# Two output parts to a pass, and conditioning loads spread evenly between the weight loads, in the first half of a gated short-convolution layer

## The chip, the cores and the metric

The kernel runs on one core of one Trainium2 chip. The number that counts is the device time of one execution in microseconds. Three timed executions of the kernel before took 926.06, 925.84 and 923.97 us, so the median is 925.84 us. Another execution was recorded by the hardware profiler; its span, from the first to the last instruction, is 925.9 us. All times "at" a point are counted from the start of that span.

## The reference

One layer is computed for 256 tokens of 2048 features; everything is float32.

```
h = rmsnorm(x, norm_g)                                    # x: 256 x 2048
mod = silu(c) @ ada_w + ada_b                             # 2048 -> 3 * 2048: shift, scale, gate
h = h * (1 + scale) + shift
b_gate, c_gate, v, g = split(h @ w_in, 4)                 # w_in: 2048 x (4 * 4096)
u = causal_depthwise_conv(c_gate * v, conv_w)             # 3 taps
y = b_gate * u * silu(g)
out = rmsnorm(x + gate * (y @ w_out), final_g)            # w_out: 4096 x 2048
```

The weights are large for so few tokens: `w_in` has 134 MB, the shift and scale columns of `ada_w` 33.5 MB, its gate columns 16.8 MB and `w_out` 33.5 MB. Each is read once.

## The kernel before

**Products.** For float32 accuracy a weight tile `raw` is split into a rounded part `hi` (ScalarE, ACT, L324) and the rest `lo` (VectorE, DVE, L325), and the activations h into `hT` the same way. A product of a 128x128 weight tile is then three matmuls on TensorE (PE, L419): hi by the rounded h, hi by the rest of h, lo by the rounded h. So after its first two matmuls a pass needs `lo`, which needs `hi`, which needs the load.

**Features come in groups.** The 2048 features are 16 feature tiles (k). A tile of h can be used once its scale and shift are known, and these are sums over all of `ada_w`'s rows. They are made on DVE: each load `at` of `ada_w` (a piece of 512 KB, issued as two DMAs of 256 KB, L388) is multiplied by silu(c) and added to `gv` by two instructions (L399 for the first of a group, else L401). Eight pieces make a group of two feature tiles; the first group is made in the start-up, seven more follow while products already run. When a group's `gv` is whole, PE turns it (`tp_g`, L408), ACT sums it (L410), and `modulate` writes `hT` for these two tiles (L309 to L318).

**The early stage.** The first half of the output channels is 16 parts: 4 chunks of channels `ch` by 4 quarters `q` (the four outputs of `w_in`), each of 512 columns. A part needs all 16 feature tiles, but they come one group after another, so a part is computed in several passes: `part(ch, q, k0, k1, seed)` takes tiles k0 to k1. A pass has one PSUM tile `mm_s` (two banks; the pool of 3 such tiles fills six of the eight banks). It loads `raw_s` (L462) with up to four feature tiles by 512 columns: 1 MB, or 512 KB for two feature tiles. The pool for `raw` has three buffers of 1 MB, those for `hi` and `lo` three each, that for `at` four. At the end `keep` brings the sums to SBUF: ACT copies them (L440) when it is the part's first pass, or when the pass was seeded, that is when ACT had copied the sums so far into PSUM before it (L452); else DVE adds them (L442).

**What sets the order.** `plan()` runs on the host and lists the passes and the `ada` pieces. It keeps four running times (load, PE, DVE, ACT) with fixed costs for each, and puts a piece before a pass when its estimate says that loading has room (`fill`). The tile framework then orders the instructions of each engine by priority and by its own estimate of time; DVE's `gv` instructions have a lower priority (`later(GIVE)`), so a `lo` may pass them. Within an engine the order is then fixed. All of the weight and `ada_w` loads are issued by one queue, SyncE's (SP), in its order.

After 3072 matmuls on `mm_s` the second half of the channels follows with all features ready (`mm_b`, loads `raw` of eight feature tiles by 256 columns), then the output product (`mm_o`). These stages aren't touched by the change.

Of the kernel before, what the change touches and what calls it, by code (L numbers as in the profile page):

```python
# [13 lines left out]
P = 128  # L14
D = 2048
E = 4096
# [35 lines left out]
def plan():  # L52

# [7 lines left out]
    burst = SLOT // P  # L61

    def ada():
        nonlocal load, dve
        k0, nk, i = pieces.pop(0)
        steps.append(("ada", k0, nk, i))
        load = max(load, dve - AAHEAD) + ALOAD
        dve = max(dve, load + 2.0) + VPIECE
        if i == 4 * nk - 1:
            ready.extend([dve + ALAG] * nk)  # L70

    def products(n, need):

        nonlocal load, pe, dve, act
        load = max(load, pe - WAHEAD)
        pe = max(pe, need, load + min(n, burst) * LOAD + WLAG) + n * PRODUCTS
        load += n * LOAD
        act = max(act, load + 2.0) + n * SBLOCK
        dve = max(dve, load + 2.0) + n * VBLOCK

    def fill():

        while pieces and max(load, dve - AAHEAD) + ALOAD + burst * LOAD + WLAG < pe:
            ada()

    order = [(ch, q) for ch in range(NCH) for q in QUARTERS]
    new = list(order)
    while new or any(k < KT for k in done.values()):
        fill()
        hi = sum(r <= pe for r in ready)  # L90
        if new:
            p = new.pop(0)
            done[p] = 0
        else:
            old = [p for p in order if done[p] < KT]
            p = old[0] if hi == KT else min(old, key=lambda p: done[p])
            while hi == done[p]:
                while len(ready) == hi:
                    ada()
                pe = max(pe, ready[hi])  # L100
                hi = sum(r <= pe for r in ready)
        products((hi - done[p]) * CT, ready[hi - 1])
        seed = done[p] > 0 and act < dve
        if done[p] == 0:
            act += SCOPY
        elif seed:
            act += SSEED
        else:
            dve += VSUM
        steps.append(("mm", *p, done[p], hi, seed))  # L110
        done[p] = hi
    while pieces:
        ada()
# [4 lines left out]
def short_conv_layer(ctx: ExitStack, tc: tile.TileContext, x, c, norm_g, ada_w, ada_b, w_in, conv_w, w_out, final_g, out):  # L118
# [325 lines left out]
    def part(ch, q, k0, k1, seed):  # L444


        col = q * E + ch * CT * P
        step = SLOT // (CT * P)
        first = k0
        bank = psum.tile([P, CT, T], F32, tag="mm", name="mm_s")  # L450
        if seed:
            nc.scalar.copy(bank, acc[ch, q])  # L452
        if pieces0:
            for k in range(NK0):
                chunk_products(bank, *pieces0[k], 0, k, k0, k1, late=True)
            pieces0.clear()
            k0 = NK0
        for s0 in range(k0, k1, step):
            sk = min(step, k1 - s0)
            n = sk * CT * P  # L460
# [25 lines left out]
    LATER = (4, 7, 10)  # L486
    whole = [0] * NCH
    for kind, *step in plan():
        if kind == "ada":
            ada_piece(*step)  # L490
        else:
            ch, k1 = step[0], step[3]
            part(*step)
            if step[2] == 0 and len(acc) in LATER:
                k = 4 + 4 * LATER.index(len(acc))
                with tc.issue_after(last_mm[0].ins), behind(ended):
                    turn_x(k, k + 4)
                    if k == 4:
                        turn(rows2, 0, 96, cw)
# [206 lines left out]
```

## Time and profile before

| | |
|---|---|
| median of three timed runs | 925.84 us |
| span of the profiled execution | 925.9 us |
| PE busy | 904.4 us, 98% of the span |
| DVE busy | 613.9 us |
| ACT busy | 472.8 us |
| first matmul on `mm_s` | 26.50 us |
| end of the `mm_s` products in the chain that ended last | 394.35 us |
| loads moved by SP's queue | 226.51 MB |

A row of the grouped view names line, engine, operation, what is written and read, and a count; then the busy time, the mean of one in ns, and the time that the engine idled just before these instructions, with what ended it. In the list of waits the three numbers are the time in total, how often, and the longest. In a timeline row the first two numbers are start and duration, and a bracket tells an idle time before and what ended it. Rows of stretches give, for each engine, busy time and (x) the number of instructions that began in it, then the granted clock of TensorE as a share, the share of DMA time and the rate in GB/s.

### The profile page before, as it was taken

What the parts mean: (1) busy time and instruction counts of PE and PEld (TensorE: products, weight loads), DVE (VectorE), ACT (ScalarE), POOL (GpSimd) and SP (SyncE); (2) the same over time, 40 slices, a digit from 0 to 9 for tenths busy, and PEclk for the clock granted to TensorE, in tenths of its full rate; (3) what the DMA queues carried; (4) which work ended last, traced back from release to release, by engine and by line L of the source; (5) the groups of instructions that cost most, each with busy time, mean ns of one, the idle gap of its engine ahead of it and who ended that gap; (6) DMA issues with size and microseconds to landing.
All of it is one profiled execution on the core that took longest, in us unless ns stands there. A gap on an engine that the chain in (4) does not pass through costs nothing.

```text
span 925.9 us, 16464 instructions
## 1 busy us (share of the span) xinstructions
PE 904.4 (98%) x7119; PEld 869.6 (94%) x7119; DVE 613.9 (66%) x604; ACT 472.8 (51%) x465; POOL 0.7 (0%) x6
## 2 busy tenths in 40 slices
PE   7999899999999999999999999999999999999996
PEld 6999899999999999999999999999999988888885
DVE  5889888898486799875554455445554544545882
ACT  3787776675557856644434433443334433444333
POOL 0000000000000000000000000000000000000000
PEclk9999999999999999999999999999999999999999
DMA  9999999999895789776655665666556496566542
GB/s 314 355 367 355 367 329 338 350 365 358 268 306 186 219 297 357 243 231 201 202 186 188 199 204 184 189 199 204 183 183 195 140 348 226 186 200 205 182 137 92
DMA packets 163753, 227.66 MB, mean 246 GB/s; under 512 B 5680, under 2 KB 104160, under 8 KB 163296
## 3 DMA queue, kind: packets, MB, share of 16 engines
q1 hardware_dynamic: 163440, 226.51, 74.0%
q8 instruction: 56, 0.92, 0.4%
q14 instruction: 17, 0.14, 0.0%
q10 hardware_dynamic: 240, 0.09, 0.0%
HBM read 224.49 MB, written 2.10 MB: 245 GB/s over the span
## 4 chain that ended last, share of the span: by engine, by line
PE 88%; DMA 6%; DVE 3%; issue 1%; SPq 1%; ACT 1%; ACTq 0%; DVEq 0%
PE mm_b L419 38%; PE mm_s L419 31%; PE mm_o L604 6%; PE mm_o L605 6%; PE mm_o L603 6%; DMA at<-in_ada_w_dram 3%; DMA raw_s<-in_sc_w_in_dram 2%; DVE gv L401 1%; DVE lo L325 1%; DMA x<-in_x_dram 1%; SPq L212 0%; ACT hi L324 0%; PE ps_gate L542 0%; PE tp_g L408 0%; SPq L388 0%
## 5 line engine op out<-in xcount | busy, mean ns | idle before, releaser
L419 PE MATMUL mm_s<-hT,hi 128*128 128x256 f32 x2048 | 352.9, 278 | 0.1
L419 PE MATMUL mm_b<-hT,hi 128*128 128x256 f32 x2048 | 348.8, 276 | 0.0
L419 PEld LDWEIGHTS mm_s<-hT,hi 128*128 128x128 f32 x2048 | 310.4, 189 | 1.2 <-issue 0.5
L419 PEld LDWEIGHTS mm_b<-hT,hi 128*128 128x128 f32 x2048 | 308.4, 188 | 0.2 <-issue 0.2
L419 PE MATMUL mm_s<-hT,lo 128*128 128x256 f32 x1024 | 284.4, 279 | 6.8 <-DVE lo L325 6.7
L419 PE MATMUL mm_b<-hT,lo 128*128 128x256 f32 x1024 | 282.6, 276 | 0.0
L325 DVE TENSOR_TENSOR lo<-raw,hi 128x2048 fp32r<-128x2048 f32 (+1 forms) x66 | 148.1, 2244 | 135.1 <-ACT hi L324 135.1
L324 ACT CAST hi<-raw 128x2048 fp32r<-128x2048 f32 (+1 forms) x66 | 123.7, 1874 | 208.5 <-PE mm_b L419 150.2
L419 PEld LDWEIGHTS mm_s<-hT,lo 128*128 128x128 f32 x1024 | 193.1, 189 | 7.6 <-DVE lo L325 7.6
L419 PEld LDWEIGHTS mm_b<-hT,lo 128*128 128x128 f32 x1024 | 192.2, 188 | 0.2 <-issue 0.2
L325 DVE TENSOR_TENSOR lo<-raw_s,hi 128x2048 fp32r<-128x2048 f32 (+1 forms) x80 | 147.9, 1849 | 40.5 <-ACT hi L324 39.7
L324 ACT CAST hi<-raw_s 128x2048 fp32r<-128x2048 f32 (+1 forms) x80 | 124.6, 1557 | 67.6 <-PE mm_s L419 49.8
L325 DVE TENSOR_TENSOR lo<-raw_o,hi 128x2048 fp32r<-128x2048 f32 x32 | 73.3, 2291 | 65.1 <-ACT hi L324 65.0
L324 ACT CAST hi<-raw_o 128x2048 fp32r<-128x2048 f32 x32 | 61.0, 1907 | 107.2 <-PE mm_o L605 85.0
L604 PE MATMUL mm_o<-lo,y 128*128 128x512 f32 x256 | 99.7, 391 | 0.0
L603 PE MATMUL mm_o<-hi,y 128*128 128x512 f32 x256 | 99.3, 389 | 0.0
L605 PE MATMUL mm_o<-hi,y 128*128 128x512 f32 x256 | 99.3, 389 | 0.0
L401 DVE SCALAR_TENSOR_TENSOR gv<-at,silu_c,gv 128x512 f32<-128x512 f32 x105 | 78.6, 749 | 9.2 <-DMA at<-in_ada_w_dram 7.8
L440 ACT COPY acc<-mm_s 128x1024 f32<-128x1024 f32 x54 | 54.4, 1010 | 35.1 <-PE mm_s L419 34.9
L605 PEld LDWEIGHTS mm_o<-hi,y 128*128 128x128 f32 x256 | 48.0, 188 | 10.1 <-issue 0.2
L604 PEld LDWEIGHTS mm_o<-lo,y 128*128 128x128 f32 x256 | 48.0, 188 | 10.1 <-issue 0.2
L603 PEld LDWEIGHTS mm_o<-hi,y 128*128 128x128 f32 x256 | 48.0, 188 | 10.0
(94 smaller groups left out, 375.4 us busy)
## 6 DMA issues: line engine op xcount, KB each, us to landing
raw<-in_sc_w_in_dram SPq DMA_DIRECT2D x64, 1024.0 KB, 5.7
raw_s<-in_sc_w_in_dram SPq DMA_DIRECT2D x47, 1024.0 KB, 7.8
raw_o<-in_sc_w_out_dram SPq DMA_DIRECT2D x32, 1024.0 KB, 5.2
at<-in_ada_w_dram SPq DMA_DIRECT2D x114, 256.0 KB, 7.3
raw_s<-in_sc_w_in_dram SPq DMA_DIRECT2D x33, 512.0 KB, 5.8
at_g<-in_ada_w_dram SPq DMA_DIRECT2D x32, 512.0 KB, 8.0
at<-in_ada_w_dram SPq DMA_DIRECT2D x6, 512.0 KB, 8.8
x<-in_x_dram SPq DMA_DIRECT2D x4, 512.0 KB, 6.1
```

What stands on the lines that cost most here:

```text
L324: nc.scalar.copy(hi[:, :n], raw[:, :n])
L325: nc.vector.tensor_tensor(out=lo[:, :n], in0=raw[:, :n], in1=hi[:, :n].bitcast(F32), op=ALU.subtract)
L401: nc.vector.scalar_tensor_tensor(out=gv, in0=at4[:, i], scalar=c_k, in1=gv, op0=ALU.mult, op1=ALU.add)
L419: mm = last_mm[0] = nc.tensor.matmul(dst, w, h[:, k], start=begins and left, stop=ends, skip_group_check=True)
L440: nc.scalar.copy(acc[ch, q], bank)
L603: nc.tensor.matmul(po, yh, hi[:, o], start=opens, stop=False, skip_group_check=True)
L604: nc.tensor.matmul(po, yh, lo[:, o], start=False, stop=False, skip_group_check=True)
L605: nc.tensor.matmul(po, yl, hi[:, o], start=False, stop=ct == NCT - 1, skip_group_check=True)
```

## The change

Two neighbouring parts (the same quarter, chunks 0 and 1 or 2 and 3) go through a pass together. A pass `parts` has two PSUM tiles instead of one. Its loads take two feature tiles by 1024 columns: still 1 MB, with rows of 4 KB instead of 2 KB, and nearly every load is now of that size. Of each load, the matmuls of the first part come first and then those of the second. Only the very first quarter of chunks 0 and 1 stays two passes of one part each. The two halves of a pass are seeded apart; by the plan's table 27 half-passes are seeded, 16 are first passes and 15 are added on DVE (before: 38, 16 and 2).

The `ada` pieces are no longer put where an estimate sees room: every 1 MB load earns 1.5 pieces (`SHARE`), which stand right behind that load and its split. `fill` is gone. The three turns of x (`turn_x`) come after 4, 6 and 10 parts' first passes instead of 4, 7 and 10. `plan()` now gives passes in another order; the table is 30 passes instead of 56.

```diff
+SHARE = 1.5
...
     def products(n, need):
...
+        for s0 in range(0, n, burst):
+            sn = min(burst, n - s0)
+            load += sn * LOAD
+            act = max(act, load + 2.0) + sn * SBLOCK
+            dve = max(dve, load + 2.0) + sn * VBLOCK
+            credit += SHARE * sn / burst
+            between.append([])
+            while pieces and credit >= 1.0:
+                credit -= 1.0
+                between[-1].append(ada())
+        return between
...
-    def fill():
-
-        while pieces and max(load, dve - AAHEAD) + ALOAD + burst * LOAD + WLAG < pe:
-            ada()
-
-    order = [(ch, q) for ch in range(NCH) for q in QUARTERS]
-    new = list(order)
+    order = [((ch, ch + 1), q) for ch in range(0, NCH, 2) for q in QUARTERS]
+    new = [((0,), QUARTERS[0]), ((1,), QUARTERS[0])] + order[1:]
...
-    def part(ch, q, k0, k1, seed):
-
-
-        col = q * E + ch * CT * P
-        step = SLOT // (CT * P)
+    def parts(chs, q, k0, k1, seeds, between):
+
+        w = len(chs) * CT * P
+        col = q * E + chs[0] * CT * P
+        step = SLOT // w
         first = k0
-        bank = psum.tile([P, CT, T], F32, tag="mm", name="mm_s")
-        if seed:
-            nc.scalar.copy(bank, acc[ch, q])
+        banks = []
+        for ch, seed in zip(chs, seeds):
+            banks.append(psum.tile([P, CT, T], F32, tag="mm", name="mm_s"))
+            if seed:
+                nc.scalar.copy(banks[-1], acc[ch, q])
...
-        for s0 in range(k0, k1, step):
+        for s0, some in zip(range(k0, k1, step), between):
             sk = min(step, k1 - s0)
-            n = sk * CT * P
+            n = sk * w
             raw = raw_tile("raw_s")
             nc.sync.dma_start(
                 raw[:, :n].rearrange("p (k f) -> p k f", k=sk),
-                w_in[0, s0 * P : (s0 + sk) * P, col : col + CT * P].rearrange("(k p) f -> p k f", p=P),
+                w_in[0, s0 * P : (s0 + sk) * P, col : col + w].rearrange("(k p) f -> p k f", p=P),
             )
             hi, lo = split(raw, n)
-            for i in range(sk):
-                chunk_products(bank, hi, lo, i * CT * P, s0 + i, k0, k1, seed)
-        keep(ch, q, first, bank, seed)
+            for piece in some:
+                ada_piece(*piece)
+            for j, (bank, seed) in enumerate(zip(banks, seeds)):
+                for i in range(sk):
+                    chunk_products(bank, hi, lo, i * w + j * CT * P, s0 + i, first, k1, seed)
+        for ch, bank, seed in zip(chs, banks, seeds):
+            keep(ch, q, first, bank, seed)
```

The first place is DVE when the stage begins, from the first group-2 instruction on `gv` (128x1024 is a load of 512 KB, 128x2048 one of 1 MB). Before:

```order
L399 TENSOR_SCALAR gv<-at,silu_c 128x512
L325 TENSOR_TENSOR lo<-raw_s,hi 128x1024
L401 SCALAR_TENSOR_TENSOR gv<-at,silu_c,gv 128x512 x4
L325 TENSOR_TENSOR lo<-raw_s,hi 128x1024
L401 SCALAR_TENSOR_TENSOR gv<-at,silu_c,gv 128x512 x2
L325 TENSOR_TENSOR lo<-raw_s,hi 128x1024
```

In the changed kernel (its lines stand 11 further down):

```order
L410 TENSOR_SCALAR gv<-at,silu_c 128x512
L336 TENSOR_TENSOR lo<-raw_s,hi 128x1024
L412 SCALAR_TENSOR_TENSOR gv<-at,silu_c,gv 128x512 x5
L336 TENSOR_TENSOR lo<-raw_s,hi 128x2048
L412 SCALAR_TENSOR_TENSOR gv<-at,silu_c,gv 128x512 x2
L336 TENSOR_TENSOR lo<-raw_s,hi 128x2048
```

The second `lo` of the stage, for the third part (now the first pair), stands behind five instructions on `gv` instead of four, and it and the next are twice as wide.

The second place is DVE near the matmul on `mm_s` number 576 of 3072. Before:

```order
L399 TENSOR_SCALAR gv<-at,silu_c 128x512
L325 TENSOR_TENSOR lo<-raw_s,hi 128x1024
L401 SCALAR_TENSOR_TENSOR gv<-at,silu_c,gv 128x512 x5
L325 TENSOR_TENSOR lo<-raw_s,hi 128x2048
L401 SCALAR_TENSOR_TENSOR gv<-at,silu_c,gv 128x512
```

In the changed kernel, where the loads are for matmuls 480, 528 and 576:

```order
L336 TENSOR_TENSOR lo<-raw_s,hi 128x2048
L412 SCALAR_TENSOR_TENSOR gv<-at,silu_c,gv 128x512 x3
L336 TENSOR_TENSOR lo<-raw_s,hi 128x2048
L412 SCALAR_TENSOR_TENSOR gv<-at,silu_c,gv 128x512 x3
L336 TENSOR_TENSOR lo<-raw_s,hi 128x2048
```

Between one load's `lo` and the next there were five instructions on `gv`, behind a `lo` of half the width; now there are three, behind a `lo` of the full width.

The third place is ACT where a pair of parts gives way to the next: quarter 3 of chunks 2 and 3 (`acc23`, from the PSUM tile `mm_s_1620`), then quarter 1 of chunks 0 and 1 (one half in `mm_s_1807`, seeded). `CAST hi` is the split of a later load. Before, with single parts:

```order
L440 COPY acc21_670<-mm_s_1449 128x1024
L452 COPY mm_s_1700<-acc20_793 128x1024
L324 CAST hi_1656<-raw_s_1654 128x1024
L440 COPY acc22_708<-mm_s_1535 128x1024
L452 COPY mm_s_1797<-acc31_850 128x1024
L324 CAST hi_1704<-raw_s_1702 128x2048
```

In the changed kernel:

```order
L465 COPY mm_s_1807<-acc01_349 128x1024
L335 CAST hi_1812<-raw_s_1810 128x2048
L335 CAST hi_1896<-raw_s_1894 128x2048
L451 COPY acc23_856<-mm_s_1620 128x1024
L335 CAST hi_1961<-raw_s_1959 128x2048
```

A pass ended in a copy out of PSUM, a seed for a later pass and one split; now a pair ends in one copy on ACT (its other half is added on DVE), and the splits of the next pass's two loads stand before it.

More of the change, by code (lines that the diff above doesn't have):

```diff
@@ L92, in plan @@
             p = new.pop(0)
-            done[p] = 0
+            k0 = done[p] = 0
+            if p not in order:
+                del done[p]
+                done[order[0]] = hi
         else:
```

81 lines of the change are left out of this document (44 added, 37 removed).

## The prediction

> **What bounds the kernel now.** I read the page first, then PE's waits, then stretches of the early stage. PE is busy 98% of the span, so only what PE loses can be won.
>
> ```profile
> span 925.9 us, 16464 instructions
> PE 904.4 (98%) x7119; PEld 869.6 (94%) x7119; DVE 613.9 (66%) x604; ACT 472.8 (51%) x465; POOL 0.7 (0%) x6
> ```
>
> In the `mm_s` stage the list of PE's waits has one row, and its three parts are three rows of PE's timeline. In each, a pass has done its matmuls with `hi` and waits for `lo`.
>
> ```profile
> PE mm_s L419 <- DVE lo L325: 6.7, 3, 3.7
> 34.68 0.39 PE L419 MATMUL mm_s<-hT,lo 128*128 128x256 f32 x1 [1.09 <-DVE lo L325]
> 71.05 0.39 PE L419 MATMUL mm_s<-hT,lo 128*128 128x256 f32 x1 [1.91 <-DVE lo L325]
> 105.89 0.39 PE L419 MATMUL mm_s<-hT,lo 128*128 128x256 f32 x1 [3.69 <-DVE lo L325]
> ```
>
> The stretches show a fourth loss and the pace. PE's clock falls to half right after the longest wait, and not after the one of 1.91.
>
> ```profile
> 106.00:108.00 2.00, 2.00 (x15) 2.00 (x16) 1.61 (x4) 1.91 (x4) 0.00 (x0) 0.82 1.10 353
> 108.00:110.00 2.00, 2.00 (x11) 2.00 (x11) 2.00 (x1) 0.93 (x1) 0.00 (x0) 0.50 1.10 355
> 110.00:112.00 2.00, 2.00 (x17) 2.00 (x16) 1.51 (x3) 1.25 (x3) 0.00 (x0) 0.82 1.04 380
> ...
> 40.00:120.00 80.00, 74.25 (x630) 73.43 (x629) 71.68 (x96) 62.32 (x84) 0.00 (x0) 0.98 1.06 364
> 120.00:240.00 120.00, 120.00 (x1059) 120.00 (x1058) 101.22 (x114) 78.11 (x85) 0.00 (x0) 1.00 1.01 345
> ```
>
> The half clock costs (0.18 + 0.50 + 0.18) x 2.00 = 1.72 us. After 120 us PE has no idle time, and one matmul takes 120.00 / 1059 = 0.1133 us. So 1.09 + 1.91 + 3.69 + 1.72 = 8.4 us is all that the stage can still give.
>
> Why `lo` is late is told by DVE's timeline before the longest wait: DVE does its instructions in order, and the `lo` stands behind `gv` instructions that wait for a load of `ada_w`.
>
> ```profile
> 97.55 2.33 DVE L401 SCALAR_TENSOR_TENSOR gv<-at,silu_c,gv 128x512 f32<-128x512 f32 x3
> 102.10 1.54 DVE L401 SCALAR_TENSOR_TENSOR gv<-at,silu_c,gv 128x512 f32<-128x512 f32 x2 [2.22 <-DMA at<-in_ada_w_dram]
> 103.55 2.28 DVE L325 TENSOR_TENSOR lo<-raw_s,hi 128x2048 fp32r<-128x2048 f32 x1
> ```
>
> And that the load is late follows from the mix. From 20 to 130 us, grouped by shape:
>
> ```profile
> L401 DVE SCALAR_TENSOR_TENSOR gv<-at,silu_c,gv 128x512 f32<-128x512 f32 x61 | 45.7, 749 | 6.8 <-DMA at<-in_ada_w_dram 6.0
> L325 DVE TENSOR_TENSOR lo<-raw_s,hi 128x1024 fp32r<-128x1024 f32 x17 | 20.8, 1221 | 1.1 <-ACT hi L324 0.9
> L325 DVE TENSOR_TENSOR lo<-raw_s,hi 128x2048 fp32r<-128x2048 f32 x9 | 20.6, 2285 | 1.8 <-ACT hi L324 1.8
> L399 DVE TENSOR_SCALAR gv<-at,silu_c 128x512 f32<-128x512 f32 x5 | 2.4, 482 | 0.1
> ```
>
> The weights are 17 x 0.5 + 9 = 17.5 MB and the `gv` instructions 66, two to a piece: 33 pieces, 1.89 for each MB of weights. A MB of weights is 48 matmuls, 48 x 0.1133 = 5.44 us. In that time the queue would have to move 1.049 + 1.89 x 0.524 = 2.04 MB; at the 364 GB/s of the row 40 to 120 that takes 5.60 us. DVE would have to do two half `lo` (2.44), 3.77 instructions on `gv` (2.82) and its share of `modulate`. Per group of eight pieces, `modulate` has the small sums and two instructions on each of two feature tiles:
>
> ```profile
> L318 DVE TENSOR_TENSOR hT<-xs,hT 128x256 fp32r<-128x256 f32 x16 | 6.4, 421 | 0.1
> L315 DVE TENSOR_SCALAR xs<-xs,scale,shift 128x256 f32<-128x256 f32 x16 | 6.3, 411 | 1.5 <-ACT hT L314 1.3
> L310 DVE TENSOR_TENSOR scale<-scale,vec 128x2 f32<-128x2 f32 x8 | 1.3, 156 | 0.1
> ```
>
> That is 2 x (0.421 + 0.411) + 3 x 0.156 = 2.13 us a group (the other two small sums taken as L310's), 0.50 for 1.89 pieces, and DVE's sum is 5.76 us. Both are over 5.44: until about 120 us the stage asks for more than queue and DVE give, and PE pays in gaps.
>
> **The change part by part.** *1. The even mix.* A load now carries 1.5 pieces. Queue: (1.049 + 0.786) / 0.364 = 5.04 us. DVE: one `lo` 2.29, three `gv` 2.25, `modulate` 0.40, and the sums that DVE now adds. Those are 15 instead of 2; one takes 1.22 (below), so 13 x 1.22 = 15.9 us, and spread over some 62 loads 0.26 us each. DVE comes to 5.20 us. Both are under 5.44, so the waits of 1.91 and 3.69 and the half clock go: **-7.32 us**. At the start the mix is a bit richer: 16 pieces stand before the tenth load of 1 MB, 1.7 to a MB, which is 5.3 us on the queue and 2.29 + 2.55 + 0.45 = 5.3 on DVE, still under 5.44. The order at matmul 576 fits: three `gv` stand where five stood.
>
> *2. The first pair.* Here the change costs. The rows of the start:
>
> ```profile
> 30.38 3.11 DVE L401 SCALAR_TENSOR_TENSOR gv<-at,silu_c,gv 128x512 f32<-128x512 f32 x4
> 33.41 1.22 DVE L325 TENSOR_TENSOR lo<-raw_s,hi 128x1024 fp32r<-128x1024 f32 x1
> ...
> 31.38 0.71 ACT L289 ACTIVATE x<-x,rstd 128x512 f32<-128x512 f32 x1
> 31.99 1.04 ACT L324 CAST hi<-raw_s 128x1024 fp32r<-128x1024 f32 x1
> ```
>
> ACT is done with x at 32.0 and then casts `hi`: 1.04 us before, 1.91 now, to 33.9. DVE did four `gv` from 30.38 to the `lo` at 33.41, 0.76 each; with five the `lo` begins at 34.17, after the cast, and takes 2.29 instead of 1.22. With the 0.05 from the end of `lo` to the matmul in the rows (34.63 to 34.68), PE goes on at 34.17 + 2.29 + 0.05 = 36.51 instead of 34.68. It has by then done two matmuls more, those with `hi` of the second half, 0.23 us. **+1.6 us.** Bounds: at best 0, if DVE waits elsewhere for less than I take; at worst 3.0, if the fifth `gv` waits for its load, which now has 0.5 MB more of weights ahead of it (0.524 / 0.364 = 1.44). I take 1.6, since the four `gv` before had no wait.
>
> Does the new gap, 33.59 to 36.51 less four matmuls (0.45), so 2.5 us, halve the clock? The rows have 1.91 without and 3.69 with it: the price lies between 0 and 1.72. It is nearer the first, and cut in two by the matmuls, so I take 0. [...]
>
> *3. Fewer, larger operations*, all hidden. From the groups of the whole span:
>
> ```profile
> L324 ACT CAST hi<-raw_s 128x2048 fp32r<-128x2048 f32 x47 | 89.9, 1913 | 50.6 <-PE mm_s L419 37.9 <-DMA raw_s<-in_sc_w_in_dram 9.2 <-DVE lo L325 3.5
> L440 ACT COPY acc<-mm_s 128x1024 f32<-128x1024 f32 x54 | 54.4, 1010 | 35.1 <-PE mm_s L419 34.9
> L452 ACT COPY mm_s<-acc 128x1024 f32<-128x1024 f32 x38 | 38.6, 1015 | 2.1 <-DVE acc L442 1.4
> L442 DVE TENSOR_TENSOR acc<-mm_s,acc 128x1024 f32<-128x1024 f32 x2 | 2.4, 1219 | 0.0
> ```
>
> ACT loses 54 - 43 = 11 copies out and 38 - 27 = 11 seeds, 22 x 1.01 = 22 us, but it waited for PE 37.9 and 34.9 us already: nothing. If DVE were full, its 15.9 us of added sums would stand on the path. The 33 loads of 512 KB become 16 of 1 MB: DVE saves 16 x (2 x 1.22 - 2.29) = 2.4 us, hidden too.
>
> The queue moves the same bytes. The stage ran at 364 GB/s with 17 loads of 512 KB in it, so I take no gain from larger ones. [...]
>
> *Sum.* -7.32 + 1.6 = -5.7. The profiled execution's own time is its span, 925.9, which is the median of the three timed runs (925.84), so **920.2 us**.
>
> **The rivals.** *The gaps move* (about 925.6). The bytes of the first 120 us are nearly the same, and DVE has 5.44 - 5.20 = 0.24 us a load to spare. The row of 61 `gv` has 6.8 us of idle time before them, 0.11 each; three per load are 0.33, more than the spare 0.24. Then one wait like that at 105.89 comes back, with its clock: 920.2 + 3.69 + 1.72 = 925.6. Against it: three loads of `hi` and `lo` are buffered, 2 x 5.44 us ahead of PE.
>
> *No gap at all* (917.5): the first pair's load and split come in time, if larger loads move faster than the rate of 364 GB/s says, and all of 8.4 us is gone. Against it: ACT is busy with x to 32.0 whatever the queue does.
>
> *The turnover of PSUM* (slower, about 932). A pair holds two of three PSUM tiles, so the next pair's second half waits until the first half's sums are out. That half ends 24 matmuls, 2.72 us, before the pair does, and its tile is wanted 2.72 us into the next pair. If ACT does another split first, and that split waits for PE to end the pair, then split, copy and seed take 1.91 + 1.01 + 1.02 = 3.94 us from the pair's end: 1.22 late. Six pairs are seeded in both halves (27 seeds in 21 later pair passes), the other 22 need only 2.92 us, 0.20 late: 6 x 1.22 + 22 x 0.20 = 11.7 us, and 931.9. It decides as soon as the split of the third load ahead stands before the copy on ACT. For it: all later passes turn over that way. Against it: the rows of the third place have the splits of the next two loads before the copy, whose buffers are free earlier, and the third after it.
>
> **How the numbers follow.** This kernel's measurement tells from no change about 0.3%, that is 2.8 us: 923.1 to 928.6. Forecast 0.53, with its own range from 918 to 923 (the bounds of the first gap and of the clock); no gap 0.09; both are faster: 0.62. The gaps move: 0.20, no change. The turnover 0.12, and 0.06 for a DVE that falls behind by its 15.9 us of sums (up to 936): slower, 0.18. The range goes from 916.5 (no gap, and the 1 us by which single runs differ) to 928.5, where most of the slower cases are left out.
>
> **What would show it.** Right: PE's waits for `lo` shrink to one near 34 to 36.5 us with 2 to 3 us; granted clock 1.00 from 30 us on; the `mm_s` products end near 388.6 instead of 394.35; DVE idle time before `gv` falls below 6.8. The mix is wrong if a `lo` is late after 40 us behind a `gv` that waits for its load. The turnover is right if PE waits for ACT's copies (L451, L465). Wrong altogether: any change of the stages after `mm_s`, for which I have 0.

## The result, and the profile after

The changed kernel takes 922.73 us (median of 9 executions, 920.36 to 924.1) against 925.67 us for the kernel before (9 executions, 923.87 to 926.16). The ratio is 0.9971 with a 95% interval of 0.9961 to 0.998: a gain of 0.29%, about half of the 0.62% that the forecast of 920.2 us stood for. The time is inside the forecast's range.

The page of the changed kernel, part 1, and its waits of TensorE (PE) in the whole span (time waited in all, how often, the longest):

```profile
span 921.0 us, 16348 instructions
PE 905.1 (98%) x7119; PEld 871.3 (95%) x7119; DVE 627.0 (68%) x601; ACT 450.3 (49%) x427; POOL 0.7 (0%) x6
...
PE mm_s L430 <- DVE lo L336: 1.8, 1, 1.8
...
PE mm_s L430 <- ACT hT L325: 0.5, 1, 0.5
PE mm_s L430 <- ACT acc L451: 0.4, 1, 0.4
```

In the `mm_s` stage the 6.7 us of waits for `lo` have become one of 1.8, and two small ones have come. PE's timeline at the first pair shows where (start, duration, then the instruction; in brackets the idle time before it and what ended it):

```profile
33.67 0.28 PE L430 MATMUL mm_s<-hT,lo 128*128 128x256 f32 x1
34.07 0.50 PE L430 MATMUL mm_s<-hT,hi 128*128 128x256 f32 x2
34.97 0.50 PE L430 MATMUL mm_s<-hT,hi 128*128 128x256 f32 x2 [0.40 <-ACT acc L451]
37.23 0.58 PE L430 MATMUL mm_s<-hT,lo 128*128 128x256 f32 x1 [1.76 <-DVE lo L336]
```

Stretches of the changed kernel (length, then busy time and instructions of PE, PEld, DVE, ACT, POOL, then the granted clock, the DMA share and GB/s):

```profile
27.00:40.00 13.00, 10.71 (x65) 10.11 (x65) 11.32 (x16) 10.79 (x14) 0.00 (x0) 0.76 1.05 376
40.00:120.00 80.00, 80.00 (x704) 80.00 (x704) 69.93 (x78) 64.84 (x72) 0.00 (x0) 1.00 1.02 358
120.00:240.00 120.00, 120.00 (x1060) 120.00 (x1059) 110.21 (x126) 69.23 (x82) 0.00 (x0) 1.00 0.99 349
```

From 40 to 240 us PE is never idle and its clock is full; the forecast had a full clock from 30 us on. From 27 to 40 us the mean clock was 0.76. One half of that loss is a stretch of the start-up that ends at 30.10 us (in the first profile of before at 28.79). The following rows show the other half: the stretch of half clock, 3.41 us long, and the same length of time before it. Of the engines they show PE alone:

```profile
33.51:36.93 3.42, 1.44 (x8) 1.00 1.02 405
36.93:40.34 3.41, 3.11 (x14) 0.50 1.06 367
```

The gap of the first pair left PE busy for 1.44 of 3.42 us, and in the 3.41 us behind it the clock was half. PE worked for 3.11 us of that stretch, so it costs 3.11 / 2 = 1.55 us.

### The profile page after: what moved, and what is told of

The parts are those of the page before. It is cut to its first block, busy times and chain, and to the rows that moved or that the text cites. A ratio compares the mean times of both kernels' runs of the same rounds, so it can differ in the third digit from the quotient of the medians.

```text
span 921.0 us, 16348 instructions
## 1 busy us (share of the span) xinstructions
PE 905.1 (98%) x7119; PEld 871.3 (95%) x7119; DVE 627.0 (68%) x601; ACT 450.3 (49%) x427; POOL 0.7 (0%) x6
## 4 chain that ended last, share of the span: by engine, by line
PE 95%; DMA 3%; SPq 1%; DVE 0%; ACT 0%; ACTq 0%; issue 0%; DVEq 0%
PE mm_b L430 38%; PE mm_s L430 37%; PE mm_o L625 6%; PE mm_o L626 6%; PE mm_o L624 6%; DMA at<-in_ada_w_dram 2%; DMA x<-in_x_dram 1%; DMA raw_s<-in_sc_w_in_dram 1%; PE ps_gate L563 0%; SPq L223 0%; PE tp_g L419 0%; PE tp_x L305 0%; DVE lo L336 0%; SPq L203 0%; SPq L399 0%; ACT big L643 0%
## 5 line engine op out<-in xcount | busy, mean ns | idle before, releaser
L335 ACT CAST hi<-raw_s 128x2048 fp32r<-128x2048 f32 (+1 forms) x64 | 121.6, 1901 | 102.6 <-PE mm_s L430 88.9
L336 DVE TENSOR_TENSOR lo<-raw_s,hi 128x2048 fp32r<-128x2048 f32 (+1 forms) x64 | 145.4, 2273 | 33.2 <-ACT hi L335 30.3
L451 ACT COPY acc<-mm_s 128x1024 f32<-128x1024 f32 x43 | 43.5, 1014 | 18.1 <-PE mm_s L430 18.0
```

The lines of the kernel that those rows point to most:

```text
L335: nc.scalar.copy(hi[:, :n], raw[:, :n])
L336: nc.vector.tensor_tensor(out=lo[:, :n], in0=raw[:, :n], in1=hi[:, :n].bitcast(F32), op=ALU.subtract)
L451: nc.scalar.copy(acc[ch, q], bank)
```

## The experiments

Times are medians. "Before" is the kernel before, run on the same chip beside each group of experiments (924.82 to 925.41 us); ratios are to it, with 95% intervals. Two tables are made from the traces. The first one counts the loads that have landed by 70 us and by 115 us, of those issued after 28 us; a piece is 0.5 MB of `ada_w`.

```
                                       by 70 us              by 115 us
                                  MB of w_in   pieces    MB of w_in   pieces
before, its two profiles             6, 6     13, 12.5    13.5, 13.5  27, 27
even shares, single parts             6          13          14         27
half slots in the pairs               6         13.5        12.5        31
two buffers for pieces, before        6          9          13.5        20
shared slots, single parts            7         10.5         15         24
share 2.0                             7          10          16         24
first load split                     7.5         10         16.5        24
the change                            8         9.5          16         24
pairs, shares as before               8         10.5         16         23
all seeded                            8         9.5          16        24.5
hi first                              8          10          16         23
```

The second says when PE starts product number n of `mm_s`, counted from 0 (start times of PE's rows, us; "again" is the second profile of before):

```
n          48      96     240     338     580     720    3071
before   33.13   40.01   59.12   74.34  106.23  123.75  394.07
again    34.80   40.68   59.74   76.79  105.73  121.63  391.91
change   34.07   44.63   62.93   74.61  102.53  118.76  389.08
hi first 34.54   41.06   59.40   71.06   98.98  115.21  385.53
```

### Even shares alone, and pairs alone

Even shares with single parts:

```diff
-    order = [((ch, ch + 1), q) for ch in range(0, NCH, 2) for q in QUARTERS]
-    new = [((0,), QUARTERS[0]), ((1,), QUARTERS[0])] + order[1:]
+    order = [((ch,), q) for ch in range(NCH) for q in QUARTERS]
+    new = list(order)
...
-    turn_at = [4, 6, 10]
+    turn_at = [4, 7, 10]
```

> Alone: adaLN's loads spread evenly (1.5 to a megabyte of w_in), parts still single, loads of one feature tile by 512 columns as before. Mix theory (the gain comes from the even mix; the 1-MB loads of the pairs only cost the gap at the first pair): no TensorE wait at 71 and 106 us, no wait near 37 us beyond what the kernel before has at 34.7 us, mm_s ends 4 to 7 us earlier than in the profile before (394.35), time 4 to 6 us below before. Pairing theory (the gain comes from the larger loads and operations): the waits at 71 to 106 us stay in some form, time within 1.5 us of before.

Pairs with pieces put ahead of a pass by the old rule:

```diff
-            while pieces and credit >= 1.0:
-                credit -= 1.0
-                between[-1].append(ada())
         return between
 
+    def fill():
+        out = []
+        while pieces and max(load, dve - AAHEAD) + ALOAD + burst * LOAD + WLAG < pe:
+            out.append(ada())
+        return out
...
-        before = []
+        before = fill()
```

> Alone: pairs with loads of 1 MB, adaLN's loads not spread but put ahead of a pass by the planner's rule of before, in groups of up to 8. Mix theory: waits for lo stay at one or more places between 70 and 110 us, the first pair's gap comes on top, time 0 to 4 us above before. Pairing theory: no waits at 70 to 110 us, time 2 to 4 us below before, as with the change.

Measured: even shares alone 925.32 us, ratio 0.9999 (0.9988 to 1.001): nothing. Pairs alone 923.18 us, ratio 0.9971 (0.9961 to 0.9981): all that the change gives. PE's waits, first with even shares alone, then with pairs alone:

```profile
70.92 0.58 PE L430 MATMUL mm_s<-hT,lo 128*128 128x256 f32 x1 [1.95 <-DVE lo L336]
```

```profile
34.07 0.50 PE L433 MATMUL mm_s<-hT,hi 128*128 128x256 f32 x2 [1.20 <-ACT hi L338]
34.98 0.50 PE L433 MATMUL mm_s<-hT,hi 128*128 128x256 f32 x2 [0.41 <-ACT acc L454]
36.91 0.39 PE L433 MATMUL mm_s<-hT,lo 128*128 128x256 f32 x1 [1.43 <-DVE lo L339]
```

The wait at 71 us stays with even shares and goes with pairs. (The pairs' table without even shares also differs a little: 31 passes and 22 additions on DVE.) So the share that the table asks for isn't what gains. The first table shows that it isn't what the queue carries either: with single parts the table asks for 1.5 pieces a MB, and 13 for 6 MB, 2.2, have landed by 70 us, as before. The pieces have buffers of their own and stand ahead of their place in SP's order, which is fixed before the run: most of the way to 60 us it has one piece for each load of 0.5 MB.

The mix that the queue carried did fall as the prediction wanted, but by the pairs. By 115 us it is 1.9 to 2.0 pieces a MB with single parts, and 1.4 to 1.5 with pairs, with even shares or without, at nearly the same sum of 27 to 28 MB.

### What the loads of w_in wait for

The new theory starts from the wait list of SP's queue in the first profile of before, the row of the line that issues `raw_s`:

```profile
SPq L462 <- DVE lo L325: 133.7, 59, 7.1
```

A load of `w_in` can be issued when one of the three buffers `raw` is free, and that is when the `lo` three loads earlier is done. Times of three successive loads in a second profile of before and in the change (worked out from the trace):

```
                      issued   landed   lo done   first product with lo
before, 0.5 MB each    46.27    52.42    55.12     56.46
                       49.14    55.92    58.31     60.07
                       52.49    60.37    63.72     63.77
change, 1 MB each      37.34    46.84    52.80     56.93
                       41.61    50.86    56.67     63.25
                       44.48    53.44    61.03     69.17
```

Before, three buffers hold 1.5 MB, and one trip takes 9 to 11 us: 5.9 to 7.5 us a MB, where PE wants one every 5.44. So `lo` has no lead, 0.05 to 1.8 us, and each hitch is a wait. With 1 MB in a buffer the trip takes 15 to 17 us for 3 MB, 5.0 to 5.5 us a MB, and `lo` stands 4 to 8 us ahead. Three runs test this. In the first the pairs get 0.5 MB in each buffer:

```diff
         step = SLOT // w
+        if len(chs) == 2 and k1 <= 8:
+            step = 1
+            between = [x for b in between for x in (b, [])][: k1 - k0]
```

> The change with the pairs' loads of the passes that end at or before feature tile 8 cut in two: one feature tile by 1024 columns, 512 KB, each with its own cast, lo and slot; pairs, order of passes and shares of adaLN as in the change. Slot theory (three slots of raw hold three loads, 1.5 MB with loads of 512 KB and 3 MB with loads of 1 MB; what took the waits away is that w_in stands further ahead and adaLN's loads no longer overtake it): waits for lo of 2 to 6 us in all come back between 40 and 115 us, the queue carries about 2 pieces of adaLN to a megabyte of w_in between 40 and 66 us as in the kernel before, time 923.5 to 926. Rival (the order of passes by pairs or the even shares take the waits away): no wait after 40 us, and without the first pair's gap of 1.8 us and its half clock the time is 919 to 921.

Measured: 939.87 us, ratio 1.0159 (1.014 to 1.0179). 6 MB by 70 us, as before, and waits at many places from 68 to 194 us:

```profile
PE mm_s L430 <- DVE lo L336: 8.8, 12, 2.0
...
PE mm_s L430 <- ACT hi L335: 3.0, 5, 0.9
...
PE mm_s L430 <- ACT mm_s L468: 0.8, 1, 0.8
```

The direction is the slot theory's and the rival is out. But the waits for `lo`, 8.8 us (13 with the others), are above the 2 to 6 expected, and the time is 14 us above the expected range. The run changes two things, the bytes in a buffer and the size of the casts. The second test leaves the casts at 1024 columns and lets two single loads share a buffer:

```diff
-            raw = raw_tile("raw_s")
+            if n > SLOT // 2:
+                raw = raw_tile("raw_s")
+            elif half:
+                raw = half.pop()[:, SLOT // 2 :]
+            else:
+                half.append(raw_tile("raw_s"))
+                raw = half[0][:, : SLOT // 2]
```

> Even shares alone (single parts, 512 KB loads, as in the run before with single parts), but two loads of 512 KB share one slot of raw, so that three slots hold 3 MB; casts and lo are of 1024 columns as before. Slot theory: adaLN's loads stand as planned, 1.5 pieces to a megabyte, the waits at 71 and 106 us fall below 0.7 us in all, no gap of a pair, time 919.5 to 922.5. Rival (larger casts, fewer operations or pairs are needed): waits as in the single-part run (2.0 at 71, 1.0 at 288 us), time 924.5 to 926.

Measured: 930.45 us, ratio 1.006 (1.0041 to 1.0078). 7 MB and 10.5 pieces by 70 us, 1.5 a MB as the table asks, and the wait at 71 us is gone: that was product 314, and here the row at 72.33 is product 339. Waits behind it:

```profile
72.33 0.39 PE L430 MATMUL mm_s<-hT,lo 128*128 128x256 f32 x1 [0.23 <-DVE lo L336]
101.20 0.39 PE L430 MATMUL mm_s<-hT,lo 128*128 128x256 f32 x1 [1.01 <-DVE lo L336]
105.05 0.39 PE L430 MATMUL mm_s<-hT,lo 128*128 128x256 f32 x1 [0.83 <-DVE lo L336]
...
PE mm_s L430 <- ACT mm_s L467: 3.1, 1, 3.1
```

So the wait at 71 us goes with the bytes that the buffers hold (and with SP's order, which they change). For the later ones that isn't shown: products 578 and 602, the rows at 101.20 and 105.05, waited 0 and 0.30 us with even shares alone, and all waits for `lo` are 3.6 us in six places, against 2.8 in three there. The slot theory had expected under 0.7. The expected time was missed by 8 us, in part because a new wait came: a pass waits 3.1 us for ScalarE (ACT) to seed its PSUM tile. ACT's timeline before that product, which starts at 119.59, shows what the seed (L467) stood behind:

```profile
113.09 1.92 ACT L335 CAST hi<-raw_s 128x2048 fp32r<-128x2048 f32 x1 [1.63 <-PE mm_s L430]
114.91 1.01 ACT L451 COPY acc<-mm_s 128x1024 f32<-128x1024 f32 x1
115.81 1.90 ACT L335 CAST hi<-raw_s 128x2048 fp32r<-128x2048 f32 x1
117.61 1.02 ACT L451 COPY acc<-mm_s 128x1024 f32<-128x1024 f32 x1
118.51 1.03 ACT L467 COPY mm_s<-acc 128x1024 f32<-128x1024 f32 x1
```

This is the turnover of PSUM that the prediction had as a rival, in single parts instead of pairs. How much of the pairs' gain is their smaller number of passes (30 instead of 54) these runs don't separate.

The third test starts from the kernel before and takes pieces out of the queue instead:

```diff
-        at = adap.tile([P, ASLOT], F32, tag="at", name="at", bufs=4)
+        at = adap.tile([P, ASLOT], F32, tag="at", name="at", bufs=2)
...
-        at = adap.tile([P, ASLOT], F32, tag="at", name="at_g", bufs=4)
+        at = adap.tile([P, ASLOT], F32, tag="at", name="at_g", bufs=2)
```

> The kernel before with one number changed: two buffers for adaLN's pieces where it has four (in both places that use them); the gate's loads late in the kernel get two as well. Slot theory: loads in flight share one queue by the bytes that free buffers let stand in it; before, 3 loads of 0.5 MB of w_in against 4 pieces of 0.5 MB (43 percent w_in); with two pieces 60 percent, as 3 MB against 2 MB in the change. So by 70 us some 7.5 to 8 MB of w_in have landed instead of 6, and 9 to 10.5 pieces instead of 13; lo stands 2 us or more ahead of its first product between 40 and 70 us; the wait at 71 us is gone, and mm_s ends 1.5 to 4 us earlier than in the second profile of before (392.2) unless a wait for hT takes its place. Rival (the pairs' larger casts and fewer passes removed the waits): the wait at 71 us stays at 1.5 us or more, time within 1 us of before or above it.

Measured: 963.43 us, ratio 1.0429 (1.041 to 1.0447). `w_in` stays at 6 MB by 70 us, though only 9 pieces stand against it. The form of the theory in which bytes in flight share the queue is wrong. The group of `gv` instructions on VectorE (DVE) from 28 to 70 us shows the reason; its idle time was 2.6 us in the second profile of before:

```profile
L401 DVE SCALAR_TENSOR_TENSOR gv<-at,silu_c,gv 128x512 f32<-128x512 f32 x20 | 15.0, 750 | 11.8 <-DMA at<-in_ada_w_dram 11.6
```

With two buffers the pieces come late, DVE waits for them in its order, the `lo` behind them is late, and so the buffer of `w_in` is free as late as before. What sets the rate here is a buffer's whole trip, the wait on DVE included: the DMA share from 40 to 120 us is 0.93, where the kernel before has 1.06 and the change 1.02. In those the DMA engines have no idle share left, and the buffers can only decide how it is divided.

### The first pair's gap and its half clock

Products with `hi` first, in the first three pairs:

```diff
-            for j, (bank, seed) in enumerate(zip(banks, seeds)):
-                for i in range(sk):
-                    chunk_products(bank, hi, lo, i * w + j * CT * P, s0 + i, first, k1, seed)
+            first_pair = (chs, s0) == ((0, 1), 0)
+            for only in ((0, 1), (2,)) if first_pair else ((0, 1, 2),):
+                for j, (bank, seed) in enumerate(zip(banks, seeds)):
+                    for i in range(sk):
+                        chunk_products(bank, hi, lo, i * w + j * CT * P, s0 + i, first, k1, seed, only=only)
```

> The change, with the first three pairs' products in another order: all 32 products with hi, then the 16 with lo. [...] First-gap theory (the 1-MB load's long way through the cast and lo costs 1.8 us of waiting and, in most executions, a half-clock stretch worth 1.7 us): PE does not wait for lo at 37 us, the granted clock is 1.00 from 30 us on, mm_s ends 2 to 3.5 us before the change's 389.1, time 1.5 to 3.5 us below the change, 4.5 to 6.5 us below before. Rival (the loads themselves are late, so that any time gained is waited for at the second or third pair, whose loads land at 37.4 us and later): a wait for hi of 1 to 2 us near 38 to 45 us, time within 1 us of the change.

Idle transposes in the gap:

```diff
+            if (chs, q, s0) == ((0, 1), QUARTERS[1], 0):
+                chunk_products(banks[0], hi, lo, 0, 0, first, k1, ms=(0, 1), only=(0, 1))
+                keep_warm(12)
+                chunk_products(banks[0], hi, lo, 0, 0, first, k1, ms=(0, 1), only=(2,))
+                chunk_products(banks[0], hi, lo, 0, 0, first, k1, ms=(2, 3))
```

> The change, with 12 idle transposes on TensorE after the first pair's first four products, in the gap in which it waits for lo; nothing else. If the gap brings the half clock: the wait for lo is filled, lo's products still go on near 37.2 us, but at clock 1.00, mm_s ends 1.7 us earlier (387.4), time 1 to 1.7 us below the change (what the share of disturbed executions gives) and the granted clock of nearly all runs is 0.996 or more. If the half clock at 36.9 us has another cause (a fixed time since the start, or the change's other work): the clock falls as before, time within 0.5 us of the change.

Measured: `hi` first 919.15 us, ratio 0.9932 (0.9919 to 0.9945), 3.6 us below the change. It beats both kernels. Idle transposes 920.68 us, ratio 0.9948 (0.9935 to 0.9961), 2.05 below the change, and its six executions lie within 1.04 us of each other, where the change's nine spread over 3.7. With `hi` first PE has no idle time left from 27 us on, and no half clock after the start:

```profile
27.00:40.00 13.00, 13.00 (x96) 12.94 (x95) 12.32 (x16) 11.66 (x15) 0.00 (x0) 0.84 1.06 376
40.00:120.00 80.00, 80.00 (x707) 80.00 (x706) 69.80 (x80) 67.02 (x83) 0.00 (x0) 1.00 1.01 357
```

With the transposes PE works through the gap, and the first product with `lo` comes near its old time, 36.80 instead of 37.23. From 37.15 on products follow each other every 0.12 us; in the change, at half clock, it is 0.21 from 37.61 on:

```profile
34.73 0.62 PE L430 MATMUL mm_s<-hT,hi 128*128 128x256 f32 x4
35.19 1.47 PE L460 MATMUL tp_warm<-ident 128*128 128x128 f32 x12
36.41 0.48 PE L430 MATMUL mm_s<-hT,hi 128*128 128x256 f32 x2
36.80 0.51 PE L430 MATMUL mm_s<-hT,lo 128*128 128x256 f32 x2
```

These transposes do nothing but keep PE busy, so most of their 2 us is the price of the half clock (0.4 us is the earlier `lo`), and the rest to 3.6 us that of the wait itself. The rival, a wait that moves to the second pair, didn't come.

The first pair's load cut in two was the third try on this gap:

```diff
-        step = SLOT // w
+        step = 1 if (chs, q, k0) == ((0, 1), QUARTERS[1], 0) else SLOT // w
...
+        between = between + [[]] * (len(range(k0, k1, step)) - len(between))
```

> The change with the first pair's load alone cut in two loads of one feature tile by 1024 columns (512 KB), each with its own cast and lo. Step theory (TensorE pays once, where the loads step up to 1 MB, since landing, cast and lo of a 1-MB load take some 3 us longer): the wait for lo at 37 us falls below 0.8 us, and one of 1 to 2 us comes at the second pair, between 40 and 44 us, with its half clock; time 921.5 to 923.5. Rival (only the first pair's load is late, the next has time enough): no wait above 0.5 us after 38 us, time 919 to 921.

Measured: 924.49 us, ratio 0.9991 (0.9979 to 1.0003), 1.8 us worse than the change. The gap at 37 us is gone and the second pair doesn't wait; neither theory named what came instead. PE arrives earlier and waits for the features of the next group:

```profile
80.24 0.39 PE L430 MATMUL mm_s<-hT,hi 128*128 128x256 f32 x1 [2.85 <-DVE hT L329]
```

In this trace the wait cost no clock: from 40 to 120 us it was 1.00 (see the last section). The features are there at 80.52 us, in the change at 75.25. DVE's timeline shows the small sums that make them, strewn among `gv` and `lo` that stand ahead in DVE's order:

```profile
68.09 0.15 DVE L322 TENSOR_TENSOR shift<-gs,vec 128x2 f32<-128x2 f32 x1
...
72.22 0.15 DVE L320 TENSOR_TENSOR scale<-gs,b_scale 128x2 f32<-128x2 f32 x1
...
73.00 0.15 DVE L321 TENSOR_TENSOR scale<-scale,vec 128x2 f32<-128x2 f32 x1
...
78.46 0.73 DVE L326 TENSOR_SCALAR xs<-xs,scale,shift 128x256 f32<-128x256 f32 x2
...
79.77 0.75 DVE L329 TENSOR_TENSOR hT<-xs,hT 128x256 fp32r<-128x256 f32 x2
```

So the gap at the first pair was cover for the features behind it: taking the gap away gains only if those come in time, as they do with `hi` first (75.44).

### The kernel before once more

> The kernel before, unchanged, for a second profile of it: its profile in hand has a span of 925.9, longer than the spans of most of its timed runs (median 923.6, each run's time less 1.8). If that profile was a slow draw of the waits: span 922 to 924.5, the waits at 71 and 106 us together 1 to 3 us shorter than 5.6, or no half-clock stretch behind them. If the waits are fixed and only the clock differs: the same 1.9 and 3.7 us.

Measured: one execution, 925.67 us, span 923.8. Its `mm_s` waits are 0.34, 1.95 and 0.75, 3.0 us in all, against 6.7 in the first profile. The last wait in this profile, and then in the first one:

```profile
105.39 0.39 PE L419 MATMUL mm_s<-hT,lo 128*128 128x256 f32 x1 [0.75 <-DVE lo L325]
```

```profile
105.89 0.39 PE L419 MATMUL mm_s<-hT,lo 128*128 128x256 f32 x1 [3.69 <-DVE lo L325]
```

It is the same product, number 578. The `lo` comes 0.5 us apart in the two; it is PE that arrives at 104.64 in one and at 102.20 in the other. In the second profile PE had lost more on the way and waits that much less here. Up to product 48 it is 1.7 us later, as the half clock of the start-up ends at 31.69 us instead of 28.79. And a half clock right after the wait at 71.9 us, which the first profile doesn't have, costs (1 - 0.66) x 5.00 = 1.7 us:

```profile
71.90 0.38 PE L419 MATMUL mm_s<-hT,lo 128*128 128x256 f32 x1 [1.95 <-DVE lo L325]
72.00:77.00 5.00, 5.00 (x30) 5.00 (x31) 4.73 (x9) 2.05 (x2) 0.00 (x0) 0.66 1.06 372
```

So in both profiles it is the loads, and not PE, that set when the kernel before passes product 578.

### The planner's numbers

A richer share, and every later pass seeded by ACT:

```diff
-SHARE = 1.5
+SHARE = 2.0
```

> The change with SHARE 2.0 in place of 1.5. Mix theory as the prediction had it (what counts is the number of pieces per megabyte that the table asks for; at 2.0 the queue needs 5.8 us per megabyte against TensorE's 5.2 to 5.4): waits for lo of 2 us or more in all after 40 us, time 1.5 to 5 us above the change. Slot theory (the slots decide how far w_in is ahead, 3 MB against 2 MB): 7.5 to 8 MB of w_in by 70 us as with the change, lo 1 us or more ahead nearly everywhere, time within 1 us of the change.

```diff
-            seed = k0 > 0 and act < dve
+            seed = k0 > 0
```

> The change with every later pass seeded by ScalarE (the 15 additions on VectorE become 15 seeds), nothing else moved by hand. If the additions cost nothing where they stand (VectorE's lo is 3 to 7 us ahead of its use after 60 us): time within 0.7 us of the change. If they, or the banks' turnover by ScalarE, bind: waits for a seed (ScalarE) at the head of a pass, time 1 us or more above the change, or without the additions 0.7 us or more below it.

Measured: share 2.0 gives 920.55 us, ratio 0.9958 (0.9945 to 0.997), 2.2 us below the change. The theory of the prediction wanted it 1.5 to 5 us above, with 5.8 us a MB on the queue against PE's 5.44 (48 x 0.1133). But the run doesn't test the prediction's rates: the queue carried 1.4 pieces a MB by 70 us and 1.5 by 115 us, as in the change, and not 2.0. The edit did something else too: `plan()` gives 22 passes instead of 30, with 17 seeds and 9 additions instead of 27 and 15. There is no wait after 34 us; the slot theory is right on that and missed the gain. The profile shows 1.8 us of waits in place of 2.3, both in the single part one pass ahead of the first pair, and a mean granted clock of 0.993, against 0.994 in the change's profile:

```profile
32.04 0.50 PE L430 MATMUL mm_s<-hT,hi 128*128 128x256 f32 x2 [1.00 <-ACT hi L335]
33.30 0.39 PE L430 MATMUL mm_s<-hT,lo 128*128 128x256 f32 x1 [0.76 <-DVE lo L336]
```

That explains 0.5 us (the first pair, reached later, waits for nothing). Another 0.3 us comes from four small matmuls of the gate (`ps_gate`), which now stand behind the `mm_s` products: from product 720 to 3071 PE takes 2.0 us less than in the change, and from the end of the products to the end of the span 1.7 us more. The trace is of an execution of 921.76 us, 1.2 us above the median, so it can't show all of the 2.2 us, and the rest stays open. The mean granted clock of the five executions goes from 0.993 (the one of the trace) to 0.997, so a half clock that some of them don't have may be a part.

All passes seeded: 924.77 us, ratio 0.9998 (0.9989 to 1.0007), 2.0 us above the change. Its profile has waits of 1.1 us for a seed at 325 and 331 us. So the 15 additions on DVE, which the prediction took as hidden, cost nothing against seeds in their place; where the rest of the 2.0 us goes isn't shown.

Both edits that gained, together:

```diff
-SHARE = 1.5
+SHARE = 2.0
...
+            first_pair = (chs, s0) == ((0, 1), 0)
+            for only in ((0, 1), (2,)) if first_pair else ((0, 1, 2),):
...
```

> Both edits that gained: products with hi first in the first three pairs, and SHARE 2.0. If the first pair's gap with its half clock is all that the change left in the stage (the run with hi first alone had no wait after 30 us), the richer share adds nothing: time 918.5 to 919.8, as with hi first alone (919.15). If the richer share gains by itself (its run was 2 us below the change with 1.8 us of gaps left): 916.5 to 918.

Measured: 920.76 us, ratio 0.996 (0.9947 to 0.9974), neither of the two: `hi` first has lost 1.6 us.

```profile
32.24 0.50 PE L430 MATMUL mm_s<-hT,hi 128*128 128x256 f32 x2 [1.48 <-ACT hi L335]
33.50 0.39 PE L430 MATMUL mm_s<-hT,lo 128*128 128x256 f32 x1 [0.76 <-DVE lo L336]
```

At 2.0 a piece stands ahead of the first load of `raw_s`, and now `hi` and `lo` of the single part ahead of the first pair are late, which the new order of products doesn't cover. Product 720 starts at 116.58 us instead of 115.21. `hi` first with the share of 1.5 stays the best version.

## Why the prediction was right or wrong

**Right: what the change removes, in size.** "All that the stage can still give" was 8.4 us, worked from the first profile of before. With `hi` first, which loses nothing, the products of `mm_s` reach number 3071 at 385.53 instead of 394.07, 8.5 us earlier. That the two sizes agree so well is luck: two more terms of 1.4 us each, which the prediction didn't have, cancel (a later start, and PE's pace, told below). And in the change the waits at 71 and 106 us and the half clock behind them do go: after 40 us PE is busy 80.00 of 80.00.

**Wrong, and the step that failed most: the base of the sum.** "The profiled execution's own time is its span, 925.9, which is the median of the three timed runs." In all runs the time is 1.7 to 2.2 us above the span (922.73 and 921.0 here; once 2.8), so that profile is of an execution of about 927.7 us, above all nine timed ones (four of the 64 later ones took longer still). This is 1.8 of the 2.5 us by which 920.2 was missed. The 7.32 us of step 1 are thus true of that execution and not of the median. In the second profile, whose 925.67 us is the median, all waits and the half clock are 3.04 + 1.7 = 4.7 us, not 8.4. Profile against profile the change gives 925.9 - 921.0 = 4.9 us, not far from the forecast's 5.7; between the medians it is 2.9. The same step also adds 1.91, 3.69 and 1.72 as if each were lost by itself; where the loads set the pace, a loss on the way shortens the next wait.

**Wrong in size: "2. The first pair", +1.6 us.** Measured in the profile are waits of 0.13 + 0.40 + 1.76 and 1.55 of half clock, less the 1.09 that before waits there: +2.75. PE went on at 37.23 instead of 36.51: a `gv` waited 0.81 us for its load. The upper bound had such a wait, of 1.44 us, but for the fifth of the five instructions; it was the second, the first of the four in the next row.

```profile
31.86 3.11 DVE L412 SCALAR_TENSOR_TENSOR gv<-at,silu_c,gv 128x512 f32<-128x512 f32 x4 [0.81 <-DMA at<-in_ada_w_dram]
34.89 2.28 DVE L336 TENSOR_TENSOR lo<-raw_s,hi 128x2048 fp32r<-128x2048 f32 x1
```

For the half clock 0 was taken and 1.72 was the other bound. Both grounds for 0 were of no use: that the gap is nearer to the 1.91 us that had no half clock, since a wait of 1.95 us has one in the second profile, and that it is cut in two by matmuls, since the gap here, cut into 0.40 and 1.76 us, has one all the same. With the base and this term put right the sum is 927.7 - 7.32 + 2.75 = 923.1, 0.4 above the measured time.

**Left out: PE's pace.** The sum counts only idle time that the list of waits shows. From product 48 to 720, less idle time and less half of the time that PE worked at half clock, PE took 82.1 us in both profiles of before and with even shares alone, 81.0 in the change and 80.7 with `hi` first, for the same matmuls. In the two profiles of before 17 and 18 of these products start 0.15 us or more after the last one, most of them some 0.2, where 0.11 is usual; in the change 8 do. So 1.1 us is won that no row of waits shows. Against the first profile a start-up that costs 0.7 us more takes most of it back. Against the second profile product 3071 comes 2.8 us earlier, and of that waits and half clock give only 0.9 (3.04 + 1.71 less 2.29 + 1.55), the pace 1.1, and the start-up, this time shorter, 0.9.

**Wrong: what makes the mix.** Even shares alone gain nothing, and pairs with the old shares gain everything. The prediction worked out a rate for queue and DVE and took the pieces to stand where the table puts them; in the traces they don't. Its rates, for the mix that the queue carried, aren't refuted: the runs with the wait at 71 us have 1.9 to 2.0 pieces a MB by 115 us, those without it 1.4 to 1.6, and half slots, with waits at many places, 2.5. But the run with two buffers for pieces has 1.5 and waits of 28 us, so the mix alone doesn't decide. The runs point to three buffers of 0.5 MB on a trip of some 10 us, which the pairs fill with 1 MB; the pairs' larger casts and fewer passes aren't separated from that. "Fewer, larger operations, all hidden" was counted by what an operation costs; what it does to the bytes in a buffer was left out.

**The rivals.** "The gaps move" is false for `lo`: lead is 4 to 8 us. "No gap at all" is what `hi` first has, with 919.15 where 917.5 was named, but by the order of the products and not by faster loads. "The turnover of PSUM" shows in the change as 0.40 us in the first pair only, but its mechanism is real: 3.1 us with single parts in shared buffers, 1.1 us where all passes are seeded. "DVE falls behind" did not come. "0 change of the stages after": product 580 to 3071 takes 286.55 us with the change and 286.18 and 287.84 before (the last with a half clock of 1.7 in it), and from the end of `mm_s` on nothing changed: 925.93 - 394.19 = 531.74 before, 920.95 - 389.19 = 531.76 after.

## What to carry to other kernels

Before a rate is worked out for a queue, count what it may hold: buffers times bytes over one trip (issue, landing, cast, the last reader) is the most that it can carry, and the waits of the issuing queue name the reader. Count in a trace what the queue carried; a share that a plan asks for need not come. A larger load in the same buffers can raise the rate (here from 5.9 to 7.5 us a MB to 5.0 to 5.5), but the first one comes later by its landing, cast and subtraction (here its `lo` was done at 37.17 instead of 34.63); order the work so that products which need only the first result fill that time. A profile is one execution: take a second one before a sum is made from waits, and don't add waits where a supply sets the pace.

## What the runs showed of the hardware

In the first profile of before and in the change the half clock came in stretches of 3.41 us: before from 25.38 to 28.79 and from 107.30 to 110.71 us, with the change from 26.69 to 30.10 and from 36.93 to 40.34; after these the clock is 1.00 up to PE's last product. Within each of the two profiles these times lie whole multiples of 3.41 us apart (23 from 28.79 to 107.30, 2 from 30.10 to 36.93).

PE was not idle throughout ahead of them. In the 3.41 us before such a stretch it was idle for 1.84 us with pairs alone (34.52 to 37.93), 1.98 in the change (33.51 to 36.93) and 2.01 in the first profile of before (103.88 to 107.30). In the start-up it was less, 1.03 in the first profile of before (21.96 to 25.37) and 0.69 in the change (23.27 to 26.68). And no half clock came behind 1.29 us of 3.41 in the first profile of before (69.76 to 73.17). So in these traces the idle time alone doesn't tell. Two gaps, in the first profile of before and in the run with the split first load:

```profile
103.88:107.30 3.42, 1.41 (x12) 1.00 1.07 364
107.30:110.71 3.41, 3.41 (x19) 0.50 1.08 358
```

```profile
75.60:79.01 3.41, 1.79 (x16) 1.00 1.04 381
79.01:82.43 3.42, 2.19 (x18) 1.00 1.07 379
```

The first gap is 3.69 us long: 1.67 us of it lie ahead of 103.88, with a clock of 1.00 behind them, and 2.01 after it, with 0.50. The second is 2.85 us long, with 1.62 us ahead of 79.01 and 1.23 after it, and cost no clock. The same wait of 1.9 us at 71 us brought a half clock in one profile of before (0.66 from 72 to 77 us) and none in the other (1.00 from 73.17 to 76.58).
